# Two-block network on one core: ways back and gathers of the experts spread over the pairs, and products on zeros in PE's gaps

## The chip, the cores and the metric

One core of a Trainium2 chip runs the whole program. Its engines work side by side: TensorE (PE, with PEld for its weight loads), VectorE (DVE), ScalarE (ACT), GpSimd (POOL) and SyncE (SP), whose queue issues the weight transfers. The metric is device time in microseconds (us) of one execution, a median over several runs. [...]

## The reference

Two networks one after the other, batch 1, 256 tokens, width 1024. The first block has two layers with modulated norms: half feed-forward (2816 wide), a mixer (neighbourhood attention and a bidirectional scan in the first layer, spatial gating in the second), half feed-forward; in the first layer the first half feed-forward is also done for 256 context tokens. The second block has two layers of attention mixer and routed experts. The routed part, cut to what matters:

```python
aff = sigmoid(x @ router_w)                       # 256 tokens, 16 experts
sel = aff + router_b                              # best group of 4 experts, then its best two
w = aff[chosen] / sum(aff[chosen])
for e in range(16):
    y += gates[:, e] * ((silu(x @ w_gate[e]) * (x @ w_up[e])) @ w_down[e])
x = layer_norm(ALPHA * x + y)
```

Every expert has 512 inner columns. All weights of all experts are read once per layer: 96 transfers of 1 MB.

## The kernel before, in words

**Order.** The kernel is written with a tile framework. The Python order gives each instruction its priority; a planner then runs through the program with its own costs and gives every engine its queue: of what is ready in its reckoning, the earliest written goes first. Each engine, and SP's queue of transfers, is then passed strictly in order. `issue_after` and `keep_in_program_order` add an edge that only fixes the order in a queue.

**Dense stages.** `down` (L197) multiplies a stage's hidden rows by an output matrix, for two tiles of 128 tokens (`NT` = 2); the sums `ys` lie in four PSUM banks (`bank`, L93, tags A to D with two buffers each). The last four of the inner blocks are done tile by tile: the first tile's, then `done(0)`, then the second's, first one half of the columns, then the other, then `done(1)`. `done` is mostly `residual` (L390), which reads the bank on DVE. `down` is called for the feed-forward blocks (`ffn`, L407), for the context rows (`ffn_context`, L436), for the output matrices of the mixers of the first block, and for the mixers of the second block (`mixed`, L1604). Between stages, `norms` (L1417) takes the norm of both tiles, and turns each with eight transposes (`turn`, `shifted`: ACT evicts a bank into `hm`, DVE makes the high part `hh` and the low part `hl`). The next projection (`projT`, L149) needs both tiles turned.

**Routing.** `moe` (L1086) calls `mixed(scored)`; `scored` (L1231) transposes the rows, multiplies them by the router's weights (`logits`) and takes the moments on DVE. What follows is a chain of small DVE operations up to `mask`, the ranks of the tokens (`rk`, L1310, four PE products), and `places` (L1107), which writes `Dg`, a matrix of zeros and ones: token by place, 64 places (`CAP`) for each of 16 experts. `gather(q)` (L1115) fetches the tokens of four experts by 32 products with `Dg` and eight evictions on ACT into `xg[q]`; it serves the pairs of experts 2q and 2q+1.

**Experts.** `experts` (L1203) goes over eight pairs (`NP`). `pair_in` (L1144) multiplies by the gate columns (g, bank A, four weight loads) and the up columns (u, bank B, four loads), two experts side by side in PE's columns; between g and u it calls `between`. Then `sg` on ACT and DVE, scaled by the gates `gs`. `pair_out` of the pair before follows (four loads, `psc` products with `DT` to bring the rows back to their tokens), then `flip` (L1167), four transposes of `sg`. `back` (L1127), called in pair 0, makes all the gates by place (`gs`, 32 products with two columns each and two DVE copies) and all the ways back (`DT`, 16 transposes of `Dg` and four ACT copies). The gathers 1, 2 and 3 are called in pairs 1, 2 and 2.

**Loads of the experts.** `Loads` (L24) issues the 96 transfers of a layer in order on SP's queue, each into the buffer that comes free next; a buffer is given back when PE has used it. M1 has 4 buffers in the first layer and 2 in the second, M2 1 and 3, M3 6; three more loads go once into tiles that later hold gathered tokens (`zone`). So 14 loads can run ahead of PE at first, and 11 buffers go round. `room_left` closes the pool that holds `xr` (the rows that the gathers read) and opens M4, two more buffers, in its room; its loads wait for the gathers' products. It is called in pair 2 behind gather 3.

Of the kernel before, what the change touches and what calls it, by code (L numbers as in the profile page):

```python
# [7 lines left out]
F32 = mybir.dt.float32  # L8
# [7 lines left out]
P = 128  # L16
T = 256
# [51 lines left out]
class Net:  # L69
# [3 lines left out]
    def __init__(self, ctx, tc, A):  # L73
        self.tc, self.nc, self.A = tc, tc.nc, A
        pool = lambda name, bufs, **k: ctx.enter_context(tc.tile_pool(name=name, bufs=bufs, **k))
        self.const = pool("const", 1)
        self.ws = ctx.enter_context(ExitStack())
        self.open_weights()
        self.xp = pool("xp", 1)
        self.sp = pool("sp", 2)  # L80
        self.ps = pool("ps", 2, space=PSUM)
        self.turns, self.st = {}, [None] * NT
        self.mtags = "AB"
        self.wf = None
        self.chain, self.queued = (), (0, 0)
        self.ident = self.load(self.const, "ident", [P, P])

# [109 lines left out]
    def down(self, wv, ks, get, done, tags="CD", pool=None, step=lambda i: None):  # L197
# [20 lines left out]
        for t in range(NT):  # L218
            for ns in ((0,), (1,)) if t == NT - 1 else ((0, 1),):
                for i in range(nk - 4, nk):  # L220
                    add(i, t, ns)
            done(t, ys[t])
# [184 lines left out]
    def ffn(self, hT, l, s, done, bg, gc=None, early=()):  # L407
# [7 lines left out]
        with self.tc.tile_pool(name="ffn", bufs=2) as fp:  # L415
# [18 lines left out]
            self.down(wo, range(NF), lambda f: gs[f], done, step=step)  # L434
# [651 lines left out]
    def moe(self, x, l, mp, load, early, mixed, probe, ahead):  # L1086
# [8 lines left out]
        with ExitStack() as ctx:  # L1095
# [31 lines left out]
            def back():  # L1127

                pg = self.bank("D", "pgs")
                for j in range(NP):  # L1130
                    for t in range(NT):
                        mm(pg[:, 2 * j:2 * j + 2], Dg[:, t, P * j:P * j + P].bitcast(F32), gates[:, t, 2 * j:2 * j + 2],
                           start=(t == 0), stop=(t == NT - 1))
                v.tensor_copy(gs[0:64], pg[0:64, 0:16:2])
                v.tensor_copy(gs[64:128], pg[64:128, 1:16:2])
                for j in range(0, NP, 2):
                    ps = self.bank("D", "pdt")
                    for i in range(2):
                        for t in range(NT):
                            nc.tensor.transpose(ps[:, T * i + P * t:T * i + P * t + P],  # L1140
                                                Dg[:, t, P * (j + i):P * (j + i) + P].bitcast(F32), self.ident)
                    nc.scalar.copy(DT[:, j:j + 2], ps.rearrange("p (i n) -> p i n", i=2))
# [60 lines left out]
            def experts(load, first, after):  # L1203
                prev = None
                for j in range(NP):
                    sg = pair_in(load, j, after.get(j, lambda: None))
# [5 lines left out]
            with ExitStack() as rt:  # L1212
# [18 lines left out]
                def scored(t, y):  # L1231
# [13 lines left out]
                    self.summed(x, t, y, logits)  # L1245
                    m, rs = self.moments(t)
                    z, mr = self.sp.tile([P, 16], F32, name="z", tag="z"), self.sp.tile([P, 1], F32, name="mr", tag="mr")
# [92 lines left out]
                def room_left():  # L1340
                    rt.close()
                    load.open(rt.enter_context(tc.tile_pool(name="m4", bufs=1, reuse_waits="tile")), M4)
                experts(load, True, {0: lambda: (back(), counts()), 1: lambda: gather(1, xr),
                                     2: lambda: (gather(2, xr), gather(3, xr), room_left())})
# [5 lines left out]
            with tc.If(left > 0):  # L1350
                with tc.tile_pool(name="r2", bufs=1) as rp:
                    xr = [rp.tile([P, NT, D], F32R, name=n) for n in ("xrh", "xrl")]
                    with tc.For_i(0, T // CAP - 1, 1):
# [6 lines left out]
                        back()  # L1360
# [3 lines left out]
                        experts(load, False, {})  # L1364
# [31 lines left out]
def emit(tc, A, out, lo=0, hi=99, dbg=None):  # L1396
# [3 lines left out]
    with ExitStack() as ctx:  # L1400
# [16 lines left out]
        def norms(xs, l, j, c, h, c0=0):  # L1417
            xn = [N.unit(xs, t) for t in range(NT)]
            for t in range(NT):
                last = N.modulate([xn[t]], l, j, c, h, c0 + P * t)  # L1420
            N.turned(*last)
# [157 lines left out]
        for l in range(2):  # L1579
            with tc.tile_pool(name="blk", bufs=1) as bp, ExitStack() as bp_:  # L1580
# [23 lines left out]
                mixed = lambda done: N.down(kview(A["w_o"][l]), ks, lambda k: (yT[0][:, k], yT[1][:, k]), done)  # L1604
# [160 lines left out]
```

## Time and profile before

| | us |
|---|---|
| median of 3 runs (2245.25 to 2248.6) | 2248.41 |
| the profiled execution | 2246.95 |
| its span, first to last instruction | 2244.8 |
| PE busy | 2103.6 (94%) |
| DVE, ACT, POOL busy | 1285.5, 836.4, 65.8 |

[...] Matmuls are pipelined, so the distance between the starts of two is what one costs, not its own duration. A row of the timeline gives start, duration, engine, line, operation, output and inputs by the program's names, shapes and count; in brackets the idle time of the engine before it and what ended it. Some matmul records are missing, so a count can be a few short. L numbers are lines of the kernel before.

### The profile page before, as it was taken

The numbers are of one execution on the slowest core, as the hardware profiler recorded it, in microseconds if no ns is written. First come the engines' busy times: TensorE is split into PE (matmuls) and PEld (weight loads), VectorE is DVE, ScalarE is ACT, GpSimd is POOL, SyncE is SP. The second block draws the span as 40 slices with busy tenths as digits, with TensorE's granted clock in tenths as the row PEclk, the third lists the DMA queues.
The fourth block names the chain that finished last, engine by engine and source line by source line (L and its number), as shares of the span: only waits on it lengthen the run. The fifth ranks groups of instructions, "written<-read, shape, count | busy, mean of one in ns | idle before, by whom it ended". The sixth has DMA issues, their size and how long they took to land. (4 is left out here: it accounts for less than half of the span.)

```text
span 2244.8 us, 30723 instructions
## 1 busy us (share of the span) xinstructions
PE 2103.6 (94%) x12156; PEld 1598.4 (71%) x12156; DVE 1285.5 (57%) x2572; ACT 836.4 (37%) x1467; POOL 65.8 (3%) x76
## 2 busy tenths in 40 slices
PE   7999999999989998999999999899999968989996
PEld 5878887886879997899897999787443338644332
DVE  5897637645578768776685655667211157641213
ACT  3222325435455444444554544364220015522000
POOL 0000000102000000000000000200000021100000
PEclk9999999999999999999999999999899989989998
DMA  8567634433248875785346554433789956278996
GB/s 322 201 239 274 242 113 152 128 117 48 76 169 311 289 267 199 283 290 204 132 169 225 199 177 169 181 113 133 286 357 420 420 225 240 93 278 334 420 419 253
DMA packets 94747, 514.47 MB, mean 229 GB/s; under 512 B 19648, under 2 KB 21056, under 8 KB 43520
## 3 DMA queue, kind: packets, MB, share of 16 engines
q1 hardware_dynamic: 88272, 502.34, 59.9%
q10 hardware_dynamic: 5168, 5.85, 0.8%
q0 software_dynamic: 1152, 4.19, 0.6%
q8 instruction: 99, 1.62, 0.3%
q14 instruction: 56, 0.46, 0.1%
HBM read 511.30 MB, written 1.05 MB: 228 GB/s over the span
## 5 line engine op out<-in xcount | busy, mean ns | idle before, releaser
L106 DVE TENSOR_TENSOR wlo<-raw,whi 128x1024 fp32r<-128x1024 f32 x421 | 514.2, 1232 | 285.4 <-ACT whi L105 282.9
L105 ACT CAST whi<-raw 128x1024 fp32r<-128x1024 f32 x421 | 434.6, 1048 | 626.6 <-PE pa L160 186.1
L160 PE MATMUL pa<-hh,whi 128*128 128x256 f32 (+1 forms) x720 | 224.0, 311 | 4.6 <-DVE hh L285 4.6
L160 PE MATMUL pa<-hl,whi 128*128 128x256 f32 (+1 forms) x720 | 223.1, 310 | 0.6 <-DVE hl L286 0.5
L160 PE MATMUL pa<-hh,wlo 128*128 128x256 f32 (+1 forms) x720 | 222.2, 309 | 0.0
L160 PE MATMUL pb<-hh,whi 128*128 128x256 f32 (+1 forms) x720 | 221.4, 308 | 0.0
L160 PE MATMUL pb<-hh,wlo 128*128 128x256 f32 (+1 forms) x720 | 221.1, 307 | 0.0
L160 PE MATMUL pb<-hl,whi 128*128 128x256 f32 (+1 forms) x720 | 220.9, 307 | 0.0
L363 DVE SCALAR_TENSOR_TENSOR macc<-rawm,cs,macc 128x512 f32<-128x512 f32 x266 | 193.2, 749 | 13.1 <-DMA rawm<-in_w_mod 9.1
L192 PE MATMUL yacc<-whi,gh 128*128 128x512 f32 x440 | 172.8, 398 | 1.3 <-ACT gate L383 1.3
L193 PE MATMUL yacc<-wlo,gh 128*128 128x512 f32 x440 | 171.6, 393 | 0.0
L1164 DVE SCALAR_TENSOR_TENSOR sg<-sg,gs,pe 128x512 f32<-128x512 f32 x16 | 12.0, 747 | 246.8 <-PE pe L1154 246.8
L160 PEld LDWEIGHTS pa<-hh,whi 128*128 128x128 f32 x720 | 138.4, 192 | 18.1 <-DVE hh L285 5.1
L160 PEld LDWEIGHTS pa<-hl,whi 128*128 128x128 f32 x720 | 138.3, 192 | 10.4 <-DVE hl L286 1.6
L1185 PE MATMUL yp<-mw,hT 128*64 128x512 f32 x512 | 138.6, 597 | 7.5 <-DMA mw<-in_w_dn 6.2
L160 PEld LDWEIGHTS pa<-hh,wlo 128*128 128x128 f32 x720 | 138.2, 192 | 6.4
L160 PEld LDWEIGHTS pb<-hh,whi 128*128 128x128 f32 x720 | 136.7, 190 | 6.2
L160 PEld LDWEIGHTS pb<-hl,whi 128*128 128x128 f32 x720 | 136.7, 190 | 6.2
L195 PE MATMUL yacc<-whi,gl 128*128 128x512 f32 x440 | 141.0, 394 | 0.0
L160 PEld LDWEIGHTS pb<-hh,wlo 128*128 128x128 f32 x720 | 136.3, 189 | 6.2
L1154 PE MATMUL pe<-mw,xgH 128*64 128x512 f32 x512 | 122.2, 597 | 8.0 <-DMA mw<-in_w_gu 8.0
L1154 PE MATMUL pe<-mw,xgY 128*64 128x512 f32 x464 | 126.1, 608 | 0.0
(469 smaller groups left out, 3706.8 us busy)
## 6 DMA issues: line engine op xcount, KB each, us to landing
mw<-in_w_gu SPq DMA_DIRECT2D x122, 1024.0 KB, 17.2
raw<-in_ffn_w_in SPq DMA_DIRECT2D x88, 1024.0 KB, 5.0
rawm<-in_w_mod SPq DMA_DIRECT2D x72, 1024.0 KB, 5.8
mw<-in_w_dn SPq DMA_DIRECT2D x64, 1024.0 KB, 15.7
raw<-in_ffn_w_out SPq DMA_DIRECT2D x55, 1024.0 KB, 5.1
raw<-in_mix_wT SPq DMA_DIRECT2D x8, 1024.0 KB, 5.1
raw<-in_sg_wR SPq DMA_DIRECT2D x8, 1024.0 KB, 5.1
raw<-in_sg_wT SPq DMA_DIRECT2D x8, 1024.0 KB, 4.9
```

The source lines that it names most:

```text
L105: self.nc.scalar.copy(hi, src)
L106: self.nc.vector.tensor_tensor(lo, src, hi.bitcast(F32), ALU.subtract)
L160: self.nc.tensor.matmul(o, w[:, k], h[:, k], start=(k == 0 and i == 0), stop=(k == nk - 1 and i == len(steps) - 1))
L192: mm(y[n], a, whi[:, cs[n]], start=first, stop=False)
L193: mm(y[n], a, wlo[:, cs[n]], start=False, stop=False)
L195: mm(y[n], b, whi[:, cs[n]], start=False, stop=last)
L363: v.scalar_tensor_tensor(o, raw[:, k], w, o, ALU.mult, ALU.add)
L1154: mm(ps[b:b + CAP], xg[j // 2][:, 4 * c + k, P * (j % 2) + b:P * (j % 2) + b + CAP], w[:, 512 * k:512 * k + 512], start=(c == 0 and k == 0 ...
L1164: v.scalar_tensor_tensor(sg, sg, gs[:, j:j + 1], pss[1], ALU.mult, ALU.mult)
L1185: mm(yp[n][b:b + CAP], hT[:, i, b:b + CAP], w[:, D * k + 512 * n:D * k + 512 * n + 512], start=(i == 0), stop=(i == 3), tile_position=(0, b))
```

## The change

- A tile `nil` of zeros (128 x 256, `F32R`) is made at the start, by two GpSimd operations.
- `busy(o, n)` issues n products of zeros with zeros, 128 x 128 by 256 columns, into the first half of a PSUM bank; nothing reads them. Each is kept behind what is written before it on PE.
- `down` issues 36 of them behind the second tile's products and ahead of `done(1)`, into the first tile's first bank. They are left out in the first feed-forward block (`gc` given) and in `mixed`. So they stand behind the context feed-forward, three feed-forward blocks and two output matrices of mixers.
- `scored` issues 56 behind the second tile's logits; `norms` 20 behind both tiles' transposes (four calls).
- `back(j)` makes gates and ways back of two pairs only; it is called in pairs 0, 2, 4 and 6, with 8 products, two DVE copies, 4 transposes and one ACT copy in each call.
- Gathers 1, 2, 3 are called in pairs 1, 3, 5, and `room_left` in pair 5.
- The one-column tile `mr` becomes a column of a 16-column tile.

```diff
+        self.nil = self.const.tile([P, T], F32R, name="nil")
+        nil = self.sp.tile([P, T], F32, name="hm", tag="hm", bufs=2)
+        self.nc.gpsimd.memset(nil, 0.0)
+        self.nc.gpsimd.tensor_copy(self.nil, nil)
...
+    def busy(self, o, n):
+
+        for _ in range(n):
+            self.tc.keep_in_program_order(self.nc.tensor.matmul(o[:, :T], self.nil[:, :P], self.nil, start=True, stop=True))
+
-    def down(self, wv, ks, get, done, tags="CD", pool=None, step=lambda i: None):
+    def down(self, wv, ks, get, done, tags="CD", pool=None, step=lambda i: None, idle=36):
...
                 for i in range(nk - 4, nk):
                     add(i, t, ns)
+            if t == NT - 1 and idle:
+                self.busy(ys[0][0], idle)
             done(t, ys[t])
...
-            self.down(wo, range(NF), lambda f: gs[f], done, step=step)
+            self.down(wo, range(NF), lambda f: gs[f], done, step=step, idle=36 if gc is None else 0)
...
-            def back():
-
-                pg = self.bank("D", "pgs")
-                for j in range(NP):
+            def back(j):
+
+                pg, ps = self.bank("D", "pgs"), self.bank("D", "pdt")
+                for i in range(2):
                     for t in range(NT):
-                        mm(pg[:, 2 * j:2 * j + 2], Dg[:, t, P * j:P * j + P].bitcast(F32), gates[:, t, 2 * j:2 * j + 2],
-                           start=(t == 0), stop=(t == NT - 1))
-                v.tensor_copy(gs[0:64], pg[0:64, 0:16:2])
-                v.tensor_copy(gs[64:128], pg[64:128, 1:16:2])
-                for j in range(0, NP, 2):
-                    ps = self.bank("D", "pdt")
-                    for i in range(2):
-                        for t in range(NT):
-                            nc.tensor.transpose(ps[:, T * i + P * t:T * i + P * t + P],
-                                                Dg[:, t, P * (j + i):P * (j + i) + P].bitcast(F32), self.ident)
-                    nc.scalar.copy(DT[:, j:j + 2], ps.rearrange("p (i n) -> p i n", i=2))
+                        mm(pg[:, 2 * i:2 * i + 2], Dg[:, t, P * (j + i):P * (j + i) + P].bitcast(F32),
+                           gates[:, t, 2 * (j + i):2 * (j + i) + 2], start=(t == 0), stop=(t == NT - 1))
+                for e in range(2):
+                    b = slice(CAP * e, CAP * e + CAP)
+                    v.tensor_copy(gs[b, j:j + 2], pg[b, e:4:2])
+                for i in range(2):
+                    for t in range(NT):
+                        nc.tensor.transpose(ps[:, T * i + P * t:T * i + P * t + P],
+                                            Dg[:, t, P * (j + i):P * (j + i) + P].bitcast(F32), self.ident)
+                nc.scalar.copy(DT[:, j:j + 2], ps.rearrange("p (i n) -> p i n", i=2))
...
                     self.summed(x, t, y, logits)
+                    if t == NT - 1:
+                        self.busy(self.bank("B", "idle"), 56)
...
-                experts(load, True, {0: lambda: (back(), counts()), 1: lambda: gather(1, xr),
-                                     2: lambda: (gather(2, xr), gather(3, xr), room_left())})
+                def between(j):
+                    if j % 2 == 0:
+                        back(j)
+                    elif j < NP - 1:
+                        gather(j // 2 + 1, xr)
+                    if j == 0:
+                        counts()
+                    if j == NP - 3:
+                        room_left()
+                experts(load, True, between)
...
                 last = N.modulate([xn[t]], l, j, c, h, c0 + P * t)
+            N.busy(N.bank("CD", "idle"), 20)
             N.turned(*last)
...
-                mixed = lambda done: N.down(kview(A["w_o"][l]), ks, lambda k: (yT[0][:, k], yT[1][:, k]), done)
+                mixed = lambda done: N.down(kview(A["w_o"][l]), ks, lambda k: (yT[0][:, k], yT[1][:, k]), done, idle=0)
```

## Rows read from the trace of the kernel before

**Rows 1.** The page: TensorE's granted clock in 40 slices, in tenths.
```profile
PEclk9999999999999999999999999999899989989998
```

**Rows 2.** Stretches of both expert stages: busy us, then clock, DMA share, GB/s.
```profile
1566.30:1583.80 17.50, 8.63 (x39) 6.99 (x39) 15.91 (x61) 4.20 (x8) 0.00 (x0) 0.61 0.99 411
1583.80:1664.70 80.90, 80.72 (x399) 37.18 (x400) 8.00 (x16) 21.56 (x39) 1.06 (x2) 0.98 0.73 287
1600.30:1609.40 9.10, 9.10 (x46) 3.50 (x44) 1.04 (x4) 1.07 (x2) 0.00 (x0) 1.00 0.11 16
1656.70:1664.70 8.00, 8.00 (x47) 4.46 (x48) 0.00 (x0) 4.14 (x8) 0.00 (x0) 1.00 0.06 13
1664.70:1817.50 152.80, 143.26 (x588) 49.14 (x583) 27.73 (x42) 13.00 (x23) 0.00 (x0) 1.00 1.01 418
1984.70:2066.70 82.00, 81.85 (x398) 37.94 (x398) 8.52 (x17) 21.57 (x39) 1.10 (x2) 0.96 0.72 285
1997.10:2007.00 9.90, 9.90 (x39) 4.57 (x40) 0.77 (x5) 2.25 (x4) 0.00 (x0) 0.70 0.02 6
2058.50:2066.70 8.20, 8.20 (x48) 4.56 (x49) 0.00 (x0) 4.14 (x8) 0.00 (x0) 1.00 0.07 8
2066.70:2219.40 152.70, 143.20 (x586) 49.18 (x582) 27.74 (x42) 13.03 (x23) 0.00 (x0) 1.00 1.01 418
```

**Rows 3.** SP's queue, first expert stage: waited for, us in total, times, longest.
```profile
SPq L50 <- PE pe L1154: 96.0, 34, 20.0
...
SPq L50 <- PE pg L1123: 15.6, 1, 15.6
```

**Rows 4.** PE's timeline, first expert stage: ranks, first gather, pair 0, flips, end.
```profile
1575.87 0.60 PE L1310 MATMUL rk<-mask,upper 128*128 128x32 f32 x2 [8.12 <-DVE mask L1304]
...
1577.99 0.41 PE L1123 MATMUL pg<-Dg,xrl 128*128 128x256 f32 x1
1578.20 0.41 PE L1123 MATMUL pg<-Dg,xrh 128*128 128x256 f32 x1
...
1584.04 0.28 PE L1123 MATMUL pg<-Dg,xrl 128*128 128x256 f32 x1
1584.16 0.28 PE L1123 MATMUL pg<-Dg,xrh 128*128 128x256 f32 x1
...
1585.41 7.08 PE L1154 MATMUL pe<-mw,xgY 128*64 128x512 f32 x30
1592.42 3.73 PE L1132 MATMUL pgs<-gates,Dg 128*128 128x2 f32 x32
...
1609.70 0.63 PE L1170 MATMUL pt<-ident,sg 128*128 128x128 f32 x4
...
1677.86 0.66 PE L1170 MATMUL pt<-ident,sg 128*128 128x128 f32 x4
...
1701.26 0.66 PE L1170 MATMUL pt<-ident,sg 128*128 128x128 f32 x4 [0.32 <-DVE x L1199]
...
1727.14 0.66 PE L1170 MATMUL pt<-ident,sg 128*128 128x128 f32 x4 [0.32 <-DVE x L1199]
...
1816.76 0.66 PE L1170 MATMUL pt<-ident,sg 128*128 128x128 f32 x4 [0.25 <-DVE x L1199]
...
1828.16 0.40 PE L1198 MATMUL psc<-yl,DT 128*128 128x512 f32 x1
```

**Rows 5.** Five stretches of products after a gap: one of them, and their sum.
```profile
1238.10:1241.40 3.30, 3.30 (x15) 3.30 (x16) 2.75 (x8) 3.09 (x7) 0.00 (x0) 0.50 0.00 0
...
sum 20.30, PE 19.89 PEld 18.69 DVE 17.14 ACT 15.28 POOL 0.00; mean PE 3.98 PEld 3.74 DVE 3.43 ACT 3.06 POOL 0.00
```

**Rows 6.** PE's timeline in the gap after the spatial gating: transposes of both tiles.
```profile
1232.00 1.09 PE L263 MATMUL ptr<-ident,xn 128*128 128x128 f32 x8 [1.99 <-DVE xn L761]
...
1235.72 1.94 PE L263 MATMUL ptr<-ident,xn 128*128 128x128 f32 x8 [2.63 <-DVE xn L761]
```

**Rows 7.** PE's timeline after the context feed-forward: the next idle time.
```profile
453.27 1.22 PE L488 MATMUL pr<-qf,rotT 128*128 128x256 f32 x2 [6.71 <-ACT qf L515]
```

More of the change, by code (lines that the diff above doesn't have):

```diff
@@ L1205, in experts @@
                 for j in range(NP):
-                    sg = pair_in(load, j, after.get(j, lambda: None))
+                    sg = pair_in(load, j, lambda: after(j))
                     if prev is not None:
@@ L1245, in scored @@
                     self.summed(x, t, y, logits)
+                    if t == NT - 1:
+                        self.busy(self.bank("B", "idle"), 56)
                     m, rs = self.moments(t)
-                    z, mr = self.sp.tile([P, 16], F32, name="z", tag="z"), self.sp.tile([P, 1], F32, name="mr", tag="mr")
+                    z, mr = self.sp.tile([P, 16], F32, name="z", tag="z"), self.sp.tile([P, 16], F32, name="mr", tag="mr")[:, 0:1]
                     v.tensor_scalar(mr, m, rs, -1.0, ALU.mult, ALU.mult)
@@ L1359, in moe @@
                             gather(q, xr)
-                        back()
+                        for j in range(0, NP, 2):
+                            back(j)
                         load = self.expert_loads(l)
@@ L1363, in moe @@
                         load.open(room, M2[l])
-                        experts(load, False, {})
+                        experts(load, False, lambda j: None)
         return gb, first
```

## The prediction

> **What bounds the kernel now.** I read the page's clock row first, then two-microsecond stretches of the whole span by engine, then the two expert stages as tables of stretches, the waits of SP's queue, PE's timeline, and last the short gaps between the dense stages.
>
> The clock row [rows 1] is at full speed nearly everywhere; the few 8s lie where PE runs out of work between stages. Through most of the span PE is busy with short gaps, so PE's own products are the limit there.
>
> The two expert stages are another matter. From 1664.7 to 1817.5 us the transfers run at 418 GB/s with a DMA share of 1.01, and from 2066.7 to 2219.4 the same [rows 2]: the expert weights arrive as fast as they can, and these parts can't shrink. But from 1583.8 to 1664.7 only 287 GB/s flow, 80.9 x (1 - 287/418) = 25.4 us of unused transfer time, and from 1984.7 to 2066.7 285 GB/s, 82.0 x (1 - 285/418) = 26.1 us. Whatever of this is filled ends the stage earlier by as much, as long as PE keeps up behind. Two holes are seen whole: 9.1 us (1600.3 to 1609.4) and 8.0 us (1656.7 to 1664.7), in the second layer 9.9 and 8.2. In them PE is 100% busy [rows 2]. SP's queue says what it waited for [rows 3]: 96.0 us in 34 waits for PE's expert products (a buffer comes free when PE has used it), and once 15.6 us for a gather's product, which is the pool M4 waiting for the gathers to finish with its room. So PE is late early on, the transfers stop, and the late part then runs at the speed of the transfers.
>
> What PE does in the first hole: pair 0's first half (g) runs from 1585.41 for 7.0 us, then 32 products with two columns take 3.73 us, transposes of the ways back follow, and pair 0's second half (u) is over only at the flip at 1609.70, 24.3 us after it began, where 14.0 us are expert products [rows 4]. In the second hole PE does two gathers. [...]
>
> **The change part by part, one expert stage.** All times are of the profiled execution: 2246.95 us, its span 2244.8; that is 1.5 under the median of the runs, 2248.41.
>
> *56 products on zeros behind the second tile's logits.* They begin when the 8.12 us gap does, at 1567.75. At 0.12 us each that is 6.7 us, over at 1574.5, 1.4 before the rank products are due at 1575.87; DVE's chain, which ends the gap, doesn't depend on them. At 0.21 us each it would be 11.8 and the ranks 3.7 late. I take 0.12, because PE comes out of dense products. Then the first gather runs at full speed: 32 x 0.12 = 3.8 us from about 1577.2 (the four rank products are shorter too) ends at 1581.0, where pair 0 now starts at 1585.4: 4.4 earlier. Bounds: 0 to 4.4; I take 4.2.
>
> *Ways back and gates per two pairs.* back(0) issues 8 of the 32 two-column products and 4 of the 16 transposes: 3.73/4 + 0.63 (the flip's four transposes) = 1.6 us. Pair 0 then lasts 7.0 + 1.6 + 0.6 for the counts + 7.0 = 16.2 us instead of 24.3: 8.1 earlier. Together flip 0 comes 12.3 earlier, at 1597.4. The three other calls land in pairs 2, 4 and 6, 1.6 us each, with switching 2.0. Each also puts two small DVE copies and one ACT copy there, beside PE.
>
> *Gathers at pairs 1, 3, 5 instead of 1, 2, 2.* PE's own pace of a pair is 23.4 us from flip 2 to 3 (some of pair 3's products stood before flip 2) and 25.9 from flip 3 to 4 [rows 4]; I take 25.6. Flip 0 to flip 2 took 68.2 us: less two pairs, 17.0 for three gathers, of which some 2 belong to pair 3's early products: 5.2 for a gather. So PE alone reaches flip 7 at 1597.4 + 7 x 25.6 + 3 x 5.2 + 3 x 2.0 = 1798.2, against 1816.76 now: 18.6 earlier. The tail behind it (11.7 to the last product at 1828.16) stays.
>
> *The transfers' side.* The first hole ends when u is used, 12.3 earlier, so its 9.1 us are covered by the four loads that flow until then. The second has no gathers in it any more, 8.0 more. The first loads wait for g, 4.2 earlier, of which I count 2.5. Sum 19.6, with 5.8 of the 25.4 left. Both sides nearly meet, so each will now and then wait for the other; I take 18.0. Second layer: 9.9 + 8.2 + 2.5 = 20.6 by the same steps; with the same allowance 18.0 again.
>
> *M4 opens at pair 5 instead of 2.* Two loads of room, 2 x 2.5 = 5.0 us (1.05 MB at 418 GB/s), are missing for three pairs. If the transfers never get 11 loads ahead this costs nothing: PE uses a pair in 25.6 us and its twelve loads take 30. Bounds 0 to 5.0 per layer; I take 0. SP's queue is passed in order, so M4's first load still stands ahead of later ones until gather 3 is done.
>
> **The gaps between dense stages.** The zeros of a down product go into the first tile's bank, so they wait until DVE has read it; DVE does that while PE still has the second tile's 24 last products to do, and I count no wait. Behind a stage's last product PE waits for a residual, a norm and two sets of transposes. [...] ACT and DVE must still evict both sets, and DVE is the busier of the two. I take 0.7 saved here and at each of two like it, 0.4 at the one before the second block, 0 before the spatial gating, where the first tile's products start alone and early and zeros are in their way. Together 2.5; bounds -6 to +10 saved. Behind the context feed-forward there is no gap: its 36 zeros push 4.3 us of projections back. PE idles 6.71 us later on, until a weight has landed [rows 7], and absorbs what doesn't reach that load's issue: 0 to 4.3 lost, I take 0.8. The zero tile's two POOL operations at the start lie where POOL does nothing: 0, and its 1 KB and the padded tiles 0 too, either way.
>
> **Sum.** 18.0 + 18.0 + 2.5 - 0.8 = 37.7 saved: 2209.3 for an execution like the profiled one, 2210.7 against the median. I say 2210.
>
> **The rivals.**
> A, M4's late room counts: the transfers are ahead by all 11 loads through pairs 3 to 5 and stop, and SP stands behind gather 3 again. For it: the 15.6 us wait [rows 3]. Against: 25.6 of PE against 30 of transfer for a pair. About 9 of the 18 go, in each layer: 2228.
> B, the planner that orders the queues hoists the gathers and ways back as soon as their operands are there, and the early pairs are as full as now. For it: DT and gates don't depend on the pair. Against: gathers 2 and 3 could have stood ahead of pair 1's expert products already and didn't. Only the clock's 4.4 per layer remains: 2236.
> C, both bounds give way: all 51.5 us of unused transfer time go, PE being faster with fewer switches. Against: PE's own sum gives 18.6. 2194.
> D, slower than before: the products on zeros don't hold the clock. Then they run at 0.21. In the expert stages 56 of them end 3.7 late, the gather stays slow, and flip 0 is 8.1 - 3.7 = 4.4 earlier; with the 6.3 that PE gains behind it, 10.7 saved per layer. In the gaps 36 end 7.6 us after the last product, at 1237.6 in the gap of [rows 6], 1.9 late for the second transposes, and 20 of 4.2 us stand ahead of a product that now follows these within 0.5: 5.6 lost at three places, some 2 at two more, 7.6 behind the context block, 28 in all. 28 - 21 = +7: 2255. It decides from a step of 0.21 us between zeros on. Against it: nothing in a PE instruction's row so far depends on its values.
> [...]
>
> **How the numbers follow.** Forecast 57%, with its own range 2197 to 2224 (each layer 13 to 23, the gaps -2 to +5); A 14%, C 12%, B 8%, D 6%; 3% for no change that can be told. A measurement of this kernel tells 0.2%, 4.5 us, from no change. Faster: 57 + 14 + 12 + 8 = 91, less 1 of B's edge: 90%; same 4%; slower 6%. The range takes in A, ends just short of B and holds about half of C: 2191 to 2235.
>
> **What would show it.** Right: granted clock 1 through the first gather, flip 0 some 12 us after the start that is now 24, the hole ahead of it gone, 418 GB/s from pair 1 on in both layers, flip 7 some 18 earlier. Wrong: a hole of transfers at pairs 3 to 5 (A), gathers side by side ahead of pair 2 (B), zeros 0.21 us apart (D), or transposes that wait for zeros and a first projection that starts later than now.

## Result and profile after

The changed kernel takes 2213.41 us (median of 4 runs, 2210.27 to 2217.02) against 2248.51 of before: ratio 0.9848, 95% interval 0.983 to 0.9865. The forecast was 2210. The profiled executions differ by 33.7 (spans 2244.8 and 2211.2). Where these lie, from the starts of the same rows of PE's timeline in both traces:

| stretch, by the row that ends it | before | after | saved in it |
|---|---|---|---|
| start to the first `down` product | 62.82 | 63.86 | -1.0 |
| first feed-forward and context, last product | 421.90 | 423.14 | -0.2 |
| to the first `pgt` product behind the context block | 457.52 | 463.42 | -4.7 |
| first mixer, last product | 659.17 | 664.27 | +0.8 |
| gap and projections to the next `down` product | 683.68 | 688.78 | 0.0 |
| second feed-forward block | 864.39 | 865.46 | +4.0 |
| gap | 889.53 | 890.46 | +0.1 |
| third feed-forward block | 1074.08 | 1072.11 | +2.9 |
| gap, spatial gating | 1229.38 | 1226.45 | +1.0 |
| gap | 1251.22 | 1247.94 | +0.3 |
| fourth feed-forward block | 1427.73 | 1418.98 | +5.5 |
| attention mixer, to the ranks | 1575.87 | 1566.98 | +0.1 |
| first expert stage, last product | 1828.16 | 1807.04 | +12.2 |
| mixer, to the ranks | 1977.28 | 1956.02 | +0.1 |
| second expert stage, last product | 2230.03 | 2195.96 | +12.8 |
| end | 2244.8 | 2211.2 | -0.4 |

The total is near the forecast, its parts are not: 25.0 in the expert stages, where 36 were forecast; 4.7 lost at the context block, where 0.8 were; and 12.4 in three feed-forward blocks, for which the prediction took 0. Not all of this is the change's: the third block saves 1.3 to 1.6 in three kernels below in which no tile moves (e3, f1, f2).

The granted clock of the page of after, to set beside [rows 1]: the 8s inside the span are gone (mean 0.982 of full speed, in before 0.971).

```profile
PEclk8999999999999999999999999999999999999998
```

Stretches of both expert stages of after, to set beside [rows 2] (length, busy us of PE, PEld, DVE, ACT, POOL with counts, granted clock, DMA share, GB/s):

```profile
1566.90:1574.90 8.00, 7.18 (x38) 6.14 (x38) 7.83 (x21) 3.42 (x7) 0.00 (x0) 0.79 0.99 410
1574.90:1610.00 35.10, 35.08 (x172) 14.78 (x172) 2.88 (x9) 8.55 (x15) 1.06 (x2) 1.00 0.80 304
1610.00:1774.00 164.00, 160.94 (x710) 63.62 (x708) 28.68 (x48) 23.61 (x42) 0.00 (x0) 1.00 1.01 419
1774.00:1782.00 8.00, 8.00 (x40) 2.66 (x38) 0.00 (x0) 0.60 (x1) 0.00 (x0) 1.00 0.55 213
1999.00:2163.00 164.00, 160.94 (x710) 63.62 (x708) 28.69 (x48) 23.62 (x42) 0.00 (x0) 1.00 1.01 419
```

The stretch at 419 GB/s begins at 1610, not at 1664.7, and lasts to 1774. Unused are now 35.1 x (1 - 304/418) = 9.6 and 8.0 x (1 - 213/418) = 3.9 us, 13.5 against 25.4. PE is busy 160.94 of the 164.0 us: both are full at once. From 1575 to 1800 PE never waits for an expert weight; in before it did for 7.1 us in this stage. SP's queue in the first expert stage (for what, us, times, longest), beside [rows 3]:

```profile
SPq L50 <- PE pe L1164: 161.6, 49, 18.6
...
SPq L50 <- PE pg L1134: 3.7, 3, 2.2
```

The 15.6 us of SP's wait for a gather, with which M4 opened, are gone. PE's timeline of the stage, beside [rows 4] (start, duration, engine, line, operation, count; in brackets the idle time before):

```profile
1558.71 6.96 PE L204 MATMUL idle<-nil 128*128 128x256 f32 x56
1566.98 0.38 PE L1322 MATMUL rk<-mask,upper 128*128 128x32 f32 x2 [1.32 <-DVE mask L1316]
...
1568.31 0.39 PE L1134 MATMUL pg<-Dg,xrh 128*128 128x256 f32 x1 [0.74 <-DVE Dg L1121]
...
1571.03 0.41 PE L1134 MATMUL pg<-Dg,xrh 128*128 128x256 f32 x1
1571.24 0.41 PE L1134 MATMUL pg<-Dg,xrl 128*128 128x256 f32 x1
...
1572.42 0.28 PE L1134 MATMUL pg<-Dg,xrl 128*128 128x256 f32 x1
1572.54 0.28 PE L1134 MATMUL pg<-Dg,xrh 128*128 128x256 f32 x1
...
1575.01 7.08 PE L1164 MATMUL pe<-mw,xgY 128*64 128x512 f32 x30
1582.02 1.05 PE L1143 MATMUL pgs<-gates,Dg 128*128 128x2 f32 x8
1592.84 0.66 PE L1180 MATMUL pt<-ident,sg 128*128 128x128 f32 x4
...
1795.64 0.66 PE L1180 MATMUL pt<-ident,sg 128*128 128x128 f32 x4 [0.25 <-DVE x L1209]
```

The zeros are 0.12 us apart. They end at 1565.7; then PE idles 1.32, does 0.6 of ranks and idles 0.74. The gather runs at 0.21 a product and goes over to 0.12 only near 1572. The same stretch by clock (third number from the end):

```profile
1558.70:1561.00 2.30, 2.30 (x21) 2.30 (x21) 2.19 (x7) 0.56 (x1) 0.00 (x0) 1.00 1.03 427
...
1569.00:1572.00 3.00, 3.00 (x16) 3.00 (x16) 3.00 (x12) 1.43 (x3) 0.00 (x0) 0.50 1.01 421
1572.00:1575.00 3.00, 3.00 (x18) 1.93 (x16) 3.00 (x7) 2.08 (x5) 0.00 (x0) 1.00 0.92 380
```

Flip 0 comes 25.9 behind the ranks, where it was 33.8 (1609.70 - 1575.87); flip 7 another 202.8 later, where it was 207.1.

And the term that was not foreseen. Six inner blocks of the fourth feed-forward block, from a `down` product to the one six blocks on, first in the kernel before, then in the changed one:

```profile
1251.22:1302.16 50.94, 50.94 (x362) 47.80 (x361) 29.63 (x33) 23.37 (x31) 0.00 (x0) 1.00 0.63 231
```
```profile
1247.94:1297.22 49.28, 49.28 (x362) 46.33 (x361) 29.87 (x34) 23.66 (x32) 0.00 (x0) 1.00 0.66 239
```

The same 362 products, the same order on PE, the clock at 1.00 in both, PE busy all the time: 8.49 us a block against 8.21. From start to start, the projection products (256 columns) of the three blocks are 0.1188 us apart on average in before (0.1187 to 0.1190 by block) and 0.1138 to 0.1149 in after. A duration in the trace doesn't show it (0.28 in both); only the starts do.

### The profile page after: what moved, and what is told of

Same layout as the page of the kernel before. It is cut to its first block, busy times and chain, and to the rows that moved or that the text cites. A ratio compares the mean times of both kernels' runs of the same rounds, so it can differ in the third digit from the quotient of the medians.

```text
span 2211.2 us, 31538 instructions
## 1 busy us (share of the span) xinstructions
PE 2114.2 (96%) x12564; PEld 1624.1 (73%) x12564; DVE 1287.6 (58%) x2584; ACT 836.2 (38%) x1467; POOL 65.4 (3%) x78
## 5 line engine op out<-in xcount | busy, mean ns | idle before, releaser
L164 PEld LDWEIGHTS pa<-hl,whi 128*128 128x128 f32 x720 | 136.6, 190 | 10.7 <-DVE hl L297 1.8
L1195 PE MATMUL yp<-mw,hT 128*64 128x512 f32 x512 | 120.0, 593 | 1.4 <-ACT hT L1182 1.4
```

Source lines behind the costliest of these rows:

```text
L164: self.nc.tensor.matmul(o, w[:, k], h[:, k], start=(k == 0 and i == 0), stop=(k == nk - 1 and i == len(steps) - 1))
L1195: mm(yp[n][b:b + CAP], hT[:, i, b:b + CAP], w[:, D * k + 512 * n:D * k + 512 * n + 512], start=(i == 0), stop=(i == 3), tile_position=(0, b))
```

## The experiments

Each run is compared with the kernel before on the same chip, so kernels that ran on different chips are set against each other by their ratios. Paces are means over start-to-start distances of projection products.

**The pace: places or zeros?** The change moves every tile behind `nil` by 1088 bytes (1024 for `nil`, 64 for the padded `mr`); the split weights of the main pool, which lie at the other end of the memory, stay. The starts of `hh` and `hl` against theirs are thus 1088 bytes off from before. First the kernel before with that and nothing else, and the changed kernel with 64 bytes more:

```diff
+        self.nil = self.const.tile([P, T], F32R, name="nil")
...
-                    z, mr = self.sp.tile([P, 16], F32, name="z", tag="z"), self.sp.tile([P, 1], F32, name="mr", tag="mr")
+                    z, mr = self.sp.tile([P, 16], F32, name="z", tag="z"), self.sp.tile([P, 16], F32, name="mr", tag="mr")[:, 0:1]
```


> The kernel before, with only the memory that the change takes: the tile nil is set aside but never written or read, and mr is padded to 16 columns. Every tile then lies where it lies in the changed kernel. Theory of places: the feed-forward products of 256 columns, 0.1187 us from one to the next in the kernel before and 0.1138 in the changed one, are paced by where their operands lie, so they come at 0.1138 here too and about 12 us go: 2236, ratio 0.9946. Rival, that the products on zeros in the gaps set the pace of the products behind them: the pace stays 0.1187 and the time at 2248, ratio 1.000.

Measured: 2231.06 against 2247.01, ratio 0.9926 (0.9909 to 0.9942), some 16 us by the medians, 12.8 in the profiled execution (expected: 12), of which 10.7 in the three feed-forward blocks. No instruction was added or taken away. The pace is 0.1145 to 0.1166 by block.

```diff
         self.nil = self.const.tile([P, T], F32R, name="nil")
+        self.pad = self.const.tile([P, 16], F32, name="pad")
```


> The changed kernel with one more unused tile of 64 bytes a partition behind nil, so that what lay 1088 bytes higher than before lies 1152 higher, a multiple of 128. Theory of places (the start of hh against that of the weights, modulo 128 bytes): the pace of feed-forward products goes back to 0.1187 and 12 us are lost, 2225, ratio 0.990 of before. Rival, that products on zeros set the pace: nothing changes, 2213, ratio 0.985.

Measured: 2226.77, ratio 0.9913 (0.9896 to 0.9929) against 0.9848, some 15 us more than the changed kernel; pace 0.1199 in all three blocks. The theory of places holds on both sides; the products on zeros, all present here, do nothing for the pace.

Two more paddings on the kernel c1 below, 32 bytes (c2, as here) and 96 (c3, with 24 columns):

```diff
         self.nil = self.const.tile([P, T], F32R, name="nil")
+        self.pad = self.const.tile([P, 8], F32, name="pad")
```

> The kernel c1 with 32 unused bytes a partition behind nil: hh and hl start 64 bytes behind a multiple of 128, the weights whi and wlo in the main pool 96 as always. If only equal places of the two operands (both 96) are slow, the pace is as in c1 (0.1138 to 0.1178): 2204. If the pace goes by the start of hh itself or by the distance in steps of 64, it is 0.1187 or another: up to 12 us later, 2216.

> The kernel c1 with 96 unused bytes a partition behind nil: hh and hl start on a multiple of 128 bytes, the weights 96 behind one. Equal places alone slow: 2204 as c1. If a start on the multiple is best, the pace is under 0.1138 or is 0.1138 throughout: some 4 to 8 us less, 2197. If it is the distance of 32 or 96 that counts against 64, slower, 2212.

Measured: 2223.26, ratio 0.99 (0.9884 to 0.9917), pace 0.1183; and 2216.21, ratio 0.9868 (0.9852 to 0.9885), pace 0.1168. "Equal places alone are slow" falls: with `hh` 64 or 0 bytes behind a multiple of 128 the pace is slower too, only 32 is fast. Against c1, on the same chip, c2 takes 16 us more, not 12 at most as expected; 4.6 of it lie between the expert stages, where kernels differ without a known cause. Six inner blocks of the fourth feed-forward block with 64, 32 and 96 bytes of padding, to set beside the two rows above:

```profile
1254.06:1305.06 51.00, 51.00 (x362) 48.06 (x361) 29.60 (x33) 23.36 (x31) 0.00 (x0) 1.00 0.65 230
```
```profile
1250.37:1301.25 50.88, 50.88 (x362) 47.59 (x361) 29.61 (x33) 23.38 (x32) 0.00 (x0) 1.00 0.64 230
```
```profile
1249.61:1300.00 50.39, 50.39 (x362) 47.12 (x361) 29.65 (x33) 23.45 (x32) 0.00 (x0) 1.00 0.66 232
```

**The pace by itself.** A first table of products from tiles of their own, ahead of the kernel:

```diff
+            for a in range(4):
+                for c in range(4):
...
+                                    o, w[p][:, 8 * a + P * k:8 * a + P * k + P], h[q][:, 8 * c + T * k:8 * c + T * k + T],
...
```


> The kernel before, with 3072 products put ahead of everything: the three passes of a projection (256 columns, weights of 128 x 128 from wh and wl, operands mh and ml) from tiles that lie on multiples of 128 bytes, read at offsets of 0, 32, 64 and 96 bytes in either operand, 16 cases of 96 products, twice over; nobody reads them. Its time is some 370 us above the kernel before and says nothing; the distance from one product to the next does, by case. Theory of places, by the distance of both operands modulo 128: 0.119 to 0.120 at equal offsets, 0.1138 at 64 apart, between them at 32 and 96 apart. Rival, the start of one operand alone: one row or one column of the table is fast. Rival, that it is no matter of two operands but of what DMA and DVE do beside: one pace for all.

Measured: 0.1177 to 0.1207; 64 apart is not fast (0.1178 and 0.1207). But the four cases with equal offsets agree within 0.05 ns, both rounds of a case within 0.15 ns (the very first case aside), and what counts is the difference of the two offsets. My tiles lay at odd distances from each other (4224 and 8320 bytes between high and low parts; 16384 and 8192 in the kernel), so each case mixed three distances. The second table uses the kernel's own addresses:

```diff
+CASES = [(32 * i, 0) for i in range(32)] + [(1088 + 32 * i, 0) for i in range(4)] + ...
...
+            mm(o, W[:, wb:wb + P], M[:, mb:mb + T], start=(i == 0), stop=(i == 3 * KD - 1))
```


> The kernel before with some 10000 products put ahead of everything, which nobody reads; its time says nothing, the distance from one product to the next does. The operands lie at the very addresses of the feed-forward blocks: weights from 147424 on (high parts) and 163808 on (low parts), the operand that hh and hl are from 52576 (before), high and low 8192 apart. Its start is moved by 0 to 992 bytes in steps of 32, then to 1088 (the changed kernel), 1120, 1152, 1184 (the three padded kernels), then both operands are moved together; last, five of these places with the order of a feed-forward block: 48 products of 256 columns, 12 of 512. Theory of distance: the pace is a function of the distance of the two starts, the same when both move together, 0.1187 at 0, 0.1138 to 0.1178 at 1088, 0.1183 at 1120, 0.1198 at 1152, 0.1168 at 1184, as in the kernels. Rival: the places make no such difference by themselves, all within 0.1175 to 0.1207 as in the first table of this kind, and the paces of the kernels come from the places together with what DVE, ACT and the transfers do beside.

Stretches of this run, one case of 192 products each (the counts have neighbours in them): `M` moved by 64, 128 and 256 bytes, by 1088, both operands by 32, and once more by 1088:

```profile
65.00:86.70 21.70, 21.70 (x194) 21.70 (x193) 0.00 (x0) 0.00 (x0) 0.00 (x0) 1.00 0.00 1
109.50:132.50 23.00, 23.00 (x194) 23.00 (x193) 0.00 (x0) 0.00 (x0) 0.00 (x0) 1.00 0.00 1
200.80:223.50 22.70, 22.70 (x194) 22.70 (x193) 0.00 (x0) 0.00 (x0) 0.00 (x0) 1.00 0.00 1
746.60:769.20 22.60, 22.60 (x194) 22.60 (x193) 0.00 (x0) 0.00 (x0) 0.00 (x0) 1.00 0.00 1
948.10:970.90 22.80, 22.80 (x194) 22.80 (x194) 0.00 (x0) 0.00 (x0) 0.00 (x0) 1.00 0.01 1
1084.80:1106.60 21.80, 21.80 (x194) 21.80 (x193) 0.00 (x0) 0.00 (x0) 0.00 (x0) 1.00 0.01 2
```

DVE, ACT and the transfers are at rest, the clock is full, and the pace still goes from 21.7 to 23.0 us per 192. By distance from where the operands lie in the kernel before:

| moved by, bytes | 0 | 32 | 64 | 96 | 128 | 160 | 192 | 224 |
|---|---|---|---|---|---|---|---|---|
| ns from product to product | 118.7 | 117.3 | 113.4 or 117.8 | 118.3 | 120.0 | 117.8 | 117.8 | 119.9 |

The row repeats every 256 bytes up to 992, within 0.1 ns (the first two cases of the run, 120.2 and 118.6, aside); with both operands moved together by 32 to 512 it stays at 118.6 to 118.7. So the theory of distance holds, with a period of 256. 1088 is 4 x 256 + 64. At that distance there are two paces: each case keeps one of them from end to end (117.8 at 320, 576, 832 and at first at 1088; 113.4 at 64 and in the repeat at 1088). With both operands moved on from 1088 the two come again: 113.3 to 113.5 at 32, 256 and 512, 117.8 at 64 and 128. What chooses between them wasn't found; products on zeros don't, for the three blocks of the kernel c4 below, which has none ahead of them, ran at 113.8 to 114.0. In the order of a feed-forward block the five places give 118.8 (before), 113.8 (1088), 118.4, 119.8, 116.7 (1184): the paces of the five kernels, 118.8, 113.8 to 114.9, 118.3, 119.9, 116.8. The term is settled but for that choice, which leaves a range of its own: with the places alone the fourth block ran at 8.42 us an inner block, between the two rows above, and gained less than in the changed kernel.

**The zeros.**

```diff
-                def between(j):
...
+                experts(load, True, {0: lambda: (back(), counts()), 1: lambda: gather(1, xr),
+                                     2: lambda: (gather(2, xr), gather(3, xr), room_left())})
```


> The changed kernel with back whole in pair 0 and the gathers in pairs 1, 2, 2 as before; all products on zeros and the padding stay. From the changed trace: 8.9 us earlier at the first ranks and 1.5 per layer from the first gather, so some 12 in all: 2236, ratio 0.995. By the steps of the prediction it would be 2.5 - 0.8 + 2 x 4.2 = 10: 2238. If products on zeros are worth nothing by themselves and places all, 12 still, but then with the losses behind the context block (4.7) the rest must be shown in the gaps.

Measured: 2231.53, ratio 0.9936 (0.9919 to 0.9952): what the places alone give, 0.9926, with all zeros added. No difference can be told: on the whole no worth of the zeros is seen.

```diff
-            self.down(wo, range(NF), lambda f: gs[f], done, "AB", self.wf, step)
+            self.down(wo, range(NF), lambda f: gs[f], done, "AB", self.wf, step, idle=0)
...
-                        self.busy(self.bank("B", "idle"), 56)
+                        self.busy(self.bank("B", "idle"), 68)
```


> The changed kernel with no products on zeros behind the context feed-forward, and 68 instead of 56 behind the logits. If the 36 zeros there are what the context place lost, some 4.4 of the 4.7 us between the context block's last product and the first pgt product go. If the idle 1.3 + 0.7 us between the 56 zeros and the first gather are what let the clock fall, 68 end at 1566.9, just at the ranks, the gather runs at 0.12 us and pair 0 starts 2.5 earlier in each layer. Together 2213 - 4.4 - 5 = 2204, ratio 0.981. Rivals: the context loss is the tiles' new places (stays, 2208); the clock falls all the same, by the ranks alone (2209).

Measured: 2206.93, ratio 0.9837 (0.9813 to 0.9861), within the interval of the changed kernel; the two steps can be read in the trace. From the context block's last product to the first `pgt` it takes 35.8 us (before 35.6, after 40.3): the 36 zeros were the loss, places had no part in it. From the ranks to `back`'s first product it takes 13.8, 1.3 less than after, in both layers; in before it was 16.6 and 15.7. That the 68 did this is not shown. The kernel with 64 bytes more (e6) has 56 zeros and the same idle times, and it takes 13.8 as well, at a granted clock of 1.00:

```profile
1579.52 0.38 PE L1323 MATMUL rk<-mask,upper 128*128 128x32 f32 x2 [1.33 <-DVE mask L1317]
1580.85 0.38 PE L1135 MATMUL pg<-Dg,xrh 128*128 128x256 f32 x1 [0.74 <-DVE Dg L1122]
```
```profile
1580.80:1586.20 5.40, 5.35 (x34) 4.18 (x34) 5.40 (x15) 3.26 (x7) 0.00 (x0) 1.00 1.01 419
```

With 56 zeros the first gather fell to half clock (0.50) in both layers of the changed kernel and of the one with zeros only, in neither of e6; with 68 in none of the eight gathers of c1 to c4. What sets e6 apart wasn't found. What the full clock is worth can be read all the same: the expert stages save 13.5 and 14.1 in e6, 13.7 and 14.1 in c1, against 12.2 and 12.8.

```diff
-    def down(self, wv, ks, get, done, tags="CD", pool=None, step=lambda i: None, idle=36):
+    def down(self, wv, ks, get, done, tags="CD", pool=None, step=lambda i: None, idle=0):
...
-                        self.busy(self.bank("B", "idle"), 56)
+                        self.busy(self.bank("B", "idle"), 68)
...
-            N.busy(N.bank("CD", "idle"), 20)
```


> The changed kernel with 68 products on zeros behind the logits and none elsewhere: none behind output matrices, none in the norms. If the zeros in the dense gaps are worth what they seem to be in the comparison of the kernel with places alone and that with zeros and places (about 4 us, by the faster of two paces of the products behind them, and 1 in the gaps), it is about 5 slower than c1: 2209. If they cost on the whole, as between the kernel with spreading alone and the one at equal places, it is up to 2 faster: 2202.

Measured: 2201.7, ratio 0.9813 (0.9796 to 0.9829). This is the fastest of all: by the ratios some 8 us under the changed kernel (12 by the medians, of different chips), and the two intervals just don't meet (0.983 is the changed kernel's lower end). I had expected 2209 on one theory, 2202 on the other. The zeros in the dense gaps alone are what sets it apart from c1, on the same chip: 5.2 us by the medians, with intervals that overlap, so that they cost is likely and not shown. Its first gather, with 68 zeros ahead:

```profile
1547.77 8.39 PE L204 MATMUL idle<-nil 128*128 128x256 f32 x68
1556.04 0.38 PE L1322 MATMUL rk<-mask,upper 128*128 128x32 f32 x2
...
1557.37 0.39 PE L1134 MATMUL pg<-Dg,xrh 128*128 128x256 f32 x1 [0.74 <-DVE Dg L1121]
...
1558.22 0.28 PE L1134 MATMUL pg<-Dg,xrh 128*128 128x256 f32 x1
1558.34 0.28 PE L1134 MATMUL pg<-Dg,xrl 128*128 128x256 f32 x1
```

The idle 1.32 ahead of the ranks is gone, the 0.74 ahead of the gather is still there, and the gather runs at 0.12 a product. The gap after the spatial gating, first in the changed kernel, then in this one, beside [rows 6]:

```profile
1226.91 4.47 PE L204 MATMUL yacc<-nil 128*128 128x256 f32 x36
1231.22 2.10 PE L274 MATMUL ptr<-ident,xn 128*128 128x128 f32 x16
1233.07 2.63 PE L204 MATMUL idle<-nil 128*128 128x256 f32 x20
1236.46 0.39 PE L164 MATMUL pa<-hh,whi 128*128 128x256 f32 x1 [0.76 <-DVE hh L296]
```
```profile
1218.12 1.09 PE L274 MATMUL ptr<-ident,xn 128*128 128x128 f32 x8 [2.03 <-DVE xn L772]
1221.84 1.94 PE L274 MATMUL ptr<-ident,xn 128*128 128x128 f32 x8 [2.62 <-DVE xn L772]
1224.20 0.58 PE L164 MATMUL pa<-hh,whi 128*128 128x256 f32 x1 [0.42 <-DVE hh L296]
```

With zeros the first tile's transposes wait and both tiles go together; the first projection follows 10.0 us behind the last product, without them 8.7 as in before. To the next `down` product it is 21.5 with, 20.9 without, 21.8 before: what the clock gives (1.00 from 1236.4 on with zeros, in before 0.50 from 1238.1 to 1241.4) is taken back by the wait.

**The spreading.**

```diff
-                experts(load, True, {0: lambda: (back(), counts()), 1: lambda: gather(1, xr),
-                                     2: lambda: (gather(2, xr), gather(3, xr), room_left())})
+                experts(load, True, between)
```


> The kernel before with back in four calls and the gathers in pairs 1, 3, 5, and nothing else: no products on zeros, no padding. From the changed trace, 12.3 and 12.8 us per expert stage less the 1.5 that the first gather's clock gave: 10.8 + 11.3 = 22 saved, 2226, ratio 0.990. By the prediction's own steps 8.1 + 6.3 - 0.6 = 13.8 per stage, 27.6: 2221, ratio 0.988. Rival, that most of it needs the earlier start: under 8 per stage, 2232 or more. The pace of feed-forward products should stay at 0.1187.

Measured: 2223.35, ratio 0.989 (0.9873 to 0.9906). By stage 11.1 and 12.2 us: the change's 12.2 and 12.8 are the spreading and little else. (3.8 us were lost between the stages, in the second mixer, in this run's trace; that stretch varies from kernel to kernel, without a cause that I found.) Pace 0.1187 to 0.1191. Then its halves, back in four calls alone and the gathers alone:

```diff
+                def between(j):
+                    if j % 2 == 0:
+                        back(j)
+                    if j == 0:
+                        counts()
+                    if j == 1:
+                        gather(1, xr)
+                    if j == 2:
+                        gather(2, xr), gather(3, xr), room_left()
+                experts(load, True, between)
```


> The kernel before with back in four calls (pairs 0, 2, 4, 6), the gathers in pairs 1, 2, 2 as before, no zeros, no padding. If the transfers bound a stage wherever PE does not, filling the first hole alone is worth about 8 us per stage (its 9.1, and 9.9 in the second layer, less what of the second hole grows): 2232, ratio 0.993. If the two parts simply add up to what spreading alone gave (some 11.8 per stage), the rest is the gathers' part. If flip 0 is early but the second hole takes it all back: 2246.

```diff
-                experts(load, True, {0: lambda: (back(), counts()), 1: lambda: gather(1, xr),
-                                     2: lambda: (gather(2, xr), gather(3, xr), room_left())})
+                experts(load, True, {0: lambda: (back(), counts()), 1: lambda: gather(1, xr),
+                                     3: lambda: gather(2, xr), 5: lambda: (gather(3, xr), room_left())})
```


> The kernel before with the gathers in pairs 1, 3, 5 and the room left in pair 5, back whole in pair 0, no zeros, no padding. The second hole goes, 8.0 and 8.2 us, the first stays: 2231, ratio 0.993. If PE is the bound of spreading alone, this and back alone add up to more than both together gave (some 8 + 8 against 11.8 per stage); if the transfers are, to the same.

Measured: back alone 2238.3, ratio 0.9971 (0.996 to 0.9983), 4.0 and 5.1 us by stage; the gathers alone 2229.19, ratio 0.9927 (0.9911 to 0.9944), 9.1 and 8.6. Together 13.1 and 13.7 against 11.1 and 12.2 in one: more apart than in one, which by the test set beforehand speaks for PE as the bound of the two in one, though by 2.0 and 1.5 and not by 4. Back alone falls well short of the 8 that I expected. The stretch of transfers in its trace that answers to the second hole of [rows 2]:

```profile
1650.00:1662.00 12.00, 12.00 (x68) 6.32 (x68) 0.75 (x1) 4.70 (x9) 0.00 (x0) 1.00 0.12 39
```

With the first hole filled the transfers reach the two gathers of pair 2 earlier and stand 12 us in front of them instead of 8.

## Why the prediction was right, and where it was not

The time was right, 2210 against 2213, and so was the mechanism of the expert stages, though both saved less than the 13 to 23 of the prediction's own range. The sum came right by errors that cancel, which is luck.

| term | forecast | measured in the profiled execution |
|---|---|---|
| first expert stage | 18.0 | 12.2 |
| second expert stage | 18.0 | 12.8 |
| dense gaps, four | 2.5 | 0.0, 0.1, 0.3, and 0.1 in the row of the attention mixer; in c4, without zeros there, 1.2, -0.1, 0.9, -0.5 |
| context place | -0.8 | -4.7 |
| padding, new places | 0 | 12.4 in three blocks; alone 10.7 in these, 12.8 in all |

- *56 zeros, clock through the first gather* (4.2): mis-sized, 1.5 and 0.6 by layer from the ranks to `back`. In before the gather ran at 0.21 a product with a granted clock of 0.50 (1577.9 to 1583.0), at 0.12 with 1.00 from 1584 on [rows 4]. The prediction itself had the zeros end 1.4 ahead of the ranks, and then counted a full clock behind that idle time. The granted clock was 1.00 through the zeros and 0.50 from 1569 to 1572. And the price was too high at either clock: where the gather ran at full clock (e6, c1) 2.8 and 1.9 went, for from its first product to its last it takes 5.2 and not 3.8, with two expert products (1.0) in it. Rival D is refuted at 0.12 from zero to zero; in c2 the clock even came back from 0.50 to 1.00 while PE ran zeros alone.
- *back(0) instead of all*: 8.1 earlier forecast for pair 0. It lasted 17.8 (1575.01 to 1592.84) against 24.3; the 1.6 over the forecast 16.2 are products of pair 1 that the planner put ahead of flip 0 (38 stand behind the counts, where a half has 32).
- *Gathers and PE's pace*: flip 0 to flip 7 took 202.8, forecast 200.8. A pair with gather 2 or 3 takes 33.4, pairs 4 and 6 with a call of `back` 26.9, the last 25.1; I had 30.8, 27.6 and 25.6. A gather costs 8.3 (33.4 - 25.1), not the 5.2 that I took, where my own figures give 5.0 ((68.2 - 51.2 - 2)/3). PE's side was the one that decided, as its sum said: it waits for no expert weight, and the pairs from 3 on last as long in e3 and c4, to 0.1. Flip 7 is 21.1 earlier than before, 8.9 of it from ahead of the stage, so 12.2 against the forecast 18.6: 4.3 less up to flip 0, 2.0 behind it.
- *Transfers' side*: both holes went, and 13.5 of 25.4 us stay unused. "The first hole's 9.1 are covered" holds only if the second is spread too: alone, back gave 4.0.
- *M4 later*: 0, as taken; no hole at pairs 3 to 5. A new one of 3.9 stands at 1774, in pair 7's time, 1.01 of DMA share ahead of it.
- *Dense gaps*: no run shows the 0.7 and the 0.4 a gap that make up the 2.5, or the 10 of its bounds; they were estimates of mine. The runs showed 0.0, 0.1, 0.3 and 0.1. The five stretches of [rows 5] were at 0.50 or 0.51 in before. Behind these gaps of the changed kernel the projections run at 1.00 from 677.9, 1081.1 and 1236.4 on, but still at 0.50 from 880 to 882 and from 1430 to 1434, and the first tile's transposes stand behind the zeros. Without zeros there (c4) two of the four gaps are shorter by 1.2 and 0.6, two longer by 0.3 and 0.6.
- *Context place*: mis-sized by a wrong cover. The idle time that was to absorb the zeros grew by 1.5, but work that stood ahead of it in before now stands behind it:

```profile
423.60 4.48 PE L204 MATMUL yacc<-nil 128*128 128x256 f32 x36
...
453.03 1.22 PE L499 MATMUL pr<-qf,rotT 128*128 128x256 f32 x2 [8.24 <-ACT qf L526]
457.03 0.70 PE L499 MATMUL pr<-qf,rotT 128*128 128x256 f32 x2
461.39 0.70 PE L499 MATMUL pr<-qf,rotT 128*128 128x256 f32 x2
```

  The product at 453 starts as in [rows 7]. Two `pr` with their projections, done by 446 in before, now stand behind it. The reason lies in SP's queue, first before, then after with ACT's wait:

```profile
422.55 6.29 SPq L594 DMA_DIRECT2D br<-in_na_rpb  x8
435.49 0.34 SPq L136 DMA_DIRECT2D raw<-in_mix_wG  x1
```
```profile
423.79 17.40 SPq L605 DMA_DIRECT2D br<-in_na_rpb  x12
441.30 0.54 SPq L140 DMA_DIRECT2D raw<-in_mix_wG  x1
...
451.65 1.04 ACT L109 CAST whi<-raw 128x1024 fp32r<-128x1024 f32 x1 [9.74 <-DMA raw<-in_mix_wG]
```

  With the 36 zeros in its plan the planner puts twelve `br` transfers ahead of the weight `mix_wG`, not eight. It is issued 5.8 later; ACT, passed in order, waits 9.7 for it until 451.65, and the `qf` that the `pr` need stand behind it. The same order, and 6.7 and 6.5 lost, are found in the two other kernels with zeros there (zeros only, e6); the old order, and 0.4 lost at most, in e1, e3, c1 and c4. An idle time absorbs a delay only if the work pushed can still be done in it.
- *Padded tiles and 1 KB*: "0, either way" was the largest miss, 12 us, and covered the other misses.

The rivals: A fell (SP's wait for gathers is 3.7 us, not 15.6). B fell: the gathers stand in pairs 1, 3 and 5. C: more than half of the unused transfer time stayed. D would have been 2255.

## What to carry to other kernels

A change that adds or pads a tile moves all tiles behind it, and PE's pace may move with them, here by 4% (0.1188 to 0.1138 us a product): run the new places alone, and compare products start to start, before any other cause is believed. When the total fits a forecast, hold the terms against the trace one by one; here two misses of 11 and 4 us were hidden by one of 12. Products that only keep the clock up are worth no more than the slow stretch behind them, 2.8 us a gather at most here. Elsewhere they delayed work that had been early, and through the planner they reordered the transfers too (twelve `br` ahead of `mix_wG`, not eight, and 4.7 us lost).

## What the runs showed of the hardware

- In b2 the pace of a stream of 256-column products with a weight load each went with the distance between the starts of the two operands in a partition, modulo 256 bytes: 113.3 to 120.0 ns from product to product, with DVE and ACT at rest and the granted clock at 1.00.
- At one distance, 64 bytes in this count, two paces were seen, 113.4 and 117.8, each kept through a case or a good part of a stage. In the changed kernel the inner blocks of the second feed-forward block run at 113.9 up to 755 us, at 117.8 from 759 to 799, then at 113.9 again.
- 1.32 and 0.74 us of idle with 0.6 of ranks between them, behind 56 products on zeros, were followed by a stretch at half clock (0.50 from 1569 to 1572 in the changed kernel) in four cases and not in two (e6, 1.00); 0.74 alone, behind 68 and the ranks, in none of eight.
- The clock rose among products on zeros. In the second expert layer of c2 they are all that PE runs from 1959.28 to the ranks at 1969.00; the granted clock fell to 0.50 0.8 us into them and was 1.00 again from 1963.5 on:

```profile
1960.10:1963.50 3.40, 3.40 (x19) 3.40 (x18) 3.26 (x13) 1.16 (x2) 0.00 (x0) 0.50 1.00 422
1963.50:1969.00 5.50, 5.50 (x48) 5.50 (x47) 3.93 (x20) 0.00 (x0) 0.00 (x0) 1.00 1.02 427
```
